# Storing the output of a linear ReLU attention in 2 MB pairs of octets instead of 1 MB octets

## The chip, the cores and the metric

The kernel runs on one NeuronCore of a Trainium2 chip. The metric is the time of the device in microseconds (us). Before the change it is 126.73 us, the median of four executions that lie between 126.46 and 126.92 us. One further execution was taken under the hardware profiler; all the lines of a profile below come from it.

## The reference, cut to what matters

```python
def setup_inputs():
    batch, heads, seq, dim = 8, 12, 512, 64      # Q, K, V: float32, normal random numbers

def reference(Q, K, V):
    Q_feat = np.maximum(0, Q)
    K_feat = np.maximum(0, K)
    KV = np.einsum('bhkd,bhkv->bhdv', K_feat, V)
    K_sum = np.sum(K_feat, axis=2)
    numerator = np.einsum('bhqd,bhdv->bhqv', Q_feat, KV)
    denominator = np.einsum('bhqd,bhd->bhq', Q_feat, K_sum)
    return (numerator / (denominator[:, :, :, None] + 1e-10)).astype(np.float32)
```

There are 96 independent heads. Each has a 64 x 64 matrix KV and a row K_sum, made from its 512 rows of K and V; each of its 512 rows of Q is then multiplied with KV, and divided by its product with K_sum. Three float32 arrays of 12.6 MB are read, one of 12.6 MB is written.

## The kernel before, in words

Heads are taken in *octets*: eight heads at a time, twelve octets (`NO`), numbered `o`. K and V are loaded in half octets of four heads (*groups*, `g` = 2o and 2o + 1). On its 128 partitions an octet of Q has 16 partitions for each head, and each partition holds 32 consecutive rows of 64 numbers, 8 KB in DRAM; a group of K or V has 4 KB on each partition.

**Loads.** All loads but the first two groups are issued by GpSimd (`load_kv`, L92; `load_q`, L98) and change float32 to bfloat16 on the way. They stand in one list at the head of the program, in the order K, V, K, V, Q for each octet (L110 to L113). The pools `qin`, `kin` and `vin` have 7, 12 and 12 buffers. The first two groups come as float32 through the queues of SP and ACT into buffers of the pool of the output (L103 to L107).

**What is done for one octet**, by engine:

- `prep` (L133) and `prep_v` (L141), once for each group: VectorE (DVE) makes the relu of K in two masked copies (`kf`), and V in two masked copies with a column of ones (`vo`); the second copy of V is made by ACT for even groups and by DVE for odd ones.
- `mm_kv` (L148), once for each group: 16 matmuls on TensorE (PE) accumulate KV and K_sum for four heads in the PSUM tile `ps_kv`. `kvs` (L278) does both groups, and then `evac_kv` (L156): ACT copies them into `kvd`, in four instructions. There are two buffers of `kvd`, of an octet each.
- `qt` (L181): PE transposes Q (two sets of eight, `transp`), ACT takes the relu into `qt_sb` (`relu_q`, L174).
- `denom` (L207): 16 small matmuls with the K_sum columns write `ps_den`; DVE masks (`own`, L213), sums (`den`, L218) and takes the reciprocal (`rec`, L222).
- `out_t` (L193): eight matmuls in two halves give the numerator, transposed; ACT copies each half to `ot_sb` (L203).
- `backs` (L272): two times eight float32 transposes on PE (`back`, L225) bring it back to rows, and DVE multiplies each half with the reciprocals out of PSUM into `o_sb` (`norm`, L232). Then `store`.

The PSUM tiles of `out_t` and `back` share one pool of two buffers (`pou`), so a matmul of the one waits until the other's buffer has been read.

**Order.** The schedule is manual: each engine runs its instructions in the order of the program. Iteration `o` of the loop at L286 is: `kvs(o)`, `prep(2o+2)`, the `backs` of octet o - 1, `denom(o)`, `out_t(o)`, `prep(2o+3)`, `qt(o+1)`. From octet 8 on (`SAME`) `kvs(o+1)` is done ahead of `qt(o+1)`, and the `backs` are those of octet o itself. L303 to L328 are the last two octets, whose order is written out by hand; octet 11 is stored in two halves (L244).

**Stores.** All are issued by SP. Ahead of the store of octet `o` < 7, SP issues a transfer of 128 bytes from `k_sb[2(o+5)]` to `scratch` (L242): it waits until that load has landed, and all that SP issues after it waits with it. So the store of octet o goes out when K group 2(o+5) is there. The pool of the output has 7 buffers of 8 KB on each partition.

Of the kernel before, what the change touches and what calls it, by code (L numbers as in the profile page):

```python
# [10 lines left out]
def kernel(  # L11
# [7 lines left out]
    nc = tc.nc  # L19
    B, H, S, D = Q.shape  # L20
# [5 lines left out]

    R = S * 4 // P
# [6 lines left out]
    DELAY = 5  # L34
# [7 lines left out]
    def pool(name, bufs, **kw):  # L42
        return ctx.enter_context(tc.tile_pool(name=name, bufs=bufs, **kw))

    consts = pool("consts", 1)
    qin = pool("qin", 7)
    kin = pool("kin", 12)
    vin = pool("vin", 12)
    kfp = pool("kfp", 4)
    rcp = pool("rcp", 2)  # L50
    outp = pool("outp", DELAY + 2)
# [8 lines left out]

    Qr, Kr, Vr, Or = view(Q, RQ * D), view(K, R * D), view(V, R * D), view(out, RQ * D)

# [13 lines left out]
    kvf = [consts.tile([P, 8 * 2 * D1], bf16, name=f"kvd{i}") for i in range(NK)]  # L76
    kvd = [x.rearrange("p (h d) -> p h d", h=8) for x in kvf]
# [3 lines left out]
    mask_h = consts.tile([P, 8, 2], fp32, name="mask_h")  # L81

    qt_sb = [consts.tile([P, U, P], bf16, name=f"qt{i}") for i in range(NZ)]
    ps_kv = pkv.tile([P, 2, 256], fp32, name="ps_kv")

    ps_den = pde.tile([P, 2, 256], fp32, name="ps_den")
# [15 lines left out]

    for g in range(F32):  # L103
        kv = outp.tile([P, 2, R, D], fp32, name="kv_first", tag="o_sb")
        k_sb[g], v_sb[g] = kv[:, 0], kv[:, 1]
        nc.sync.dma_start(out=k_sb[g].rearrange("p r d -> p (r d)"), in_=Kr[g])
        nc.scalar.dma_start(out=v_sb[g].rearrange("p r d -> p (r d)"), in_=Vr[g])  # L107
# [23 lines left out]
    kf, ot, rec = {}, {}, {}  # L131
# [24 lines left out]
    def evac_kv(o, gs, share=False):  # L156
        for s in range(2):
            for c in range(2):
                copy = nc.vector.tensor_copy if share and c == 1 else nc.scalar.copy
                copy(  # L160
                    kvd[o % NK][64 * c:64 * c + 64, 4 * gs.start + s:4 * gs.stop:2,
                               c * D1:c * D1 + D1].rearrange(
                        "p (g t) d -> p g t d", t=2),
                    ps_kv[64 * s:64 * s + 64, gs, 0:2 * (D + 2)].rearrange(
                        "p g (t d) -> p g t d", t=2)[:, :, :, c:c + D1])
# [8 lines left out]
    def relu_q(o, i, ps, eng=None):  # L174
        to = qt_sb[o % NZ][:, i * (U // 2):(i + 1) * (U // 2)]
        if eng is nc.vector:
            nc.vector.tensor_scalar(to, ps, scalar1=0.0, scalar2=None, op0=Alu.max)
        else:
            nc.scalar.activation(to, ps, Act.Relu)  # L179
# [6 lines left out]
    def idle(n, o):  # L186
        for i in range(n):
            nc.tensor.matmul(ps_den[:, 1], ident, q_sb[o][:, 2 * i:2 * i + 2, :], start=True, stop=True,
                             skip_group_check=True)

    def out_t(o, halves=range(2)):  # L193
        if halves[0] == 0:
            ot[o] = otp.tile([P, U, 8, 16], fp32, name="ot_sb")
        q = qt_sb[o % NZ].rearrange("p u (h c) -> p u h c", h=8)
        for j in halves:
            ps = pou.tile([P, 4, U, 16], fp32, name="ps_ot", tag="ps_out")
            for i in range(4):
                h = 4 * j + i  # L200
                nc.tensor.matmul(ps[:, i], kvd[o % NK][:, h, 1:2 * D + 1], q[:, :, h, :],  # L201
                                 start=True, stop=True, skip_group_check=True)
            nc.scalar.copy(ot[o][:, :, 4 * j:4 * j + 4], ps.rearrange("p h u c -> p u h c"))  # L203
# [3 lines left out]
    def denom(o):  # L207
        ps = ps_den[:, 0].rearrange("p (u h c) -> p u h c", u=U, h=8)
        for u in range(U):
            nc.tensor.matmul(ps[:, u], qt_sb[o % NZ][:, u, :], kvd[o % NK][:, :, 0:2 * D1:2 * D1 - 1],  # L210
                             start=True, stop=True, skip_group_check=True)
        own = rcp.tile([P, U, 8, 2], fp32, name="own")
        nc.vector.scalar_tensor_tensor(  # L213
            own.rearrange("p u h c -> p u (h c)"), ps.rearrange("p u h c -> p u (h c)"), 1e-10,
            mask_h.rearrange("p h c -> p (h c)").unsqueeze(1).to_broadcast([P, U, 16]),
            op0=Alu.add, op1=Alu.mult)
        den = rcp.tile([P, RQ], fp32, name="den")
        nc.vector.tensor_reduce(out=den.rearrange("p (u c) -> p u c", c=2),  # L218
                                in_=own.rearrange("p u h c -> p u c h"), op=Alu.add,
                                axis=mybir.AxisListType.X)  # L220
        rec[o] = rcp.tile([P, RQ], fp32, name="rec")
        nc.vector.reciprocal(rec[o], den)  # L222


    def back(o, j):  # L225
        ps = pou.tile([P, 16, D], fp32, name="ps_bk", tag="ps_out")
        for v in range(8):
            nc.tensor.transpose(ps[:, 2 * v:2 * v + 2].rearrange("p c d -> p (c d)"),  # L228
                                ot[o][:, 8 * j + v].rearrange("p h c -> p (h c)"), ident32)
        return ps  # L230

    def norm(o, j, ps, o_sb):  # L232
        rs = slice(16 * j, 16 * j + 16)
        nc.vector.tensor_tensor(o_sb[:, rs], ps,  # L234
                                rec[o][:, rs].unsqueeze(2).to_broadcast([P, 16, D]), op=Alu.mult)
# [4 lines left out]
    def store(o, o_sb):  # L240
        if o + DELAY < NO:
            nc.sync.dma_start(out=scratch, in_=k_sb[2 * (o + DELAY)][0:1, 0, :])  # L242
        Ov = Or[o].rearrange("p (r d) -> p r d", d=D)
        if o == NO - 1:  # L244
            for j in range(2):
                rs = slice(RQ // 2 * j, RQ // 2 * (j + 1))
                nc.sync.dma_start(out=Ov[:, rs], in_=o_sb[:, rs])
            return
        nc.sync.dma_start(out=Ov, in_=o_sb)

    def out_tile():
        return outp.tile([P, RQ, D], fp32, name="o_sb", tag="o_sb")
# [7 lines left out]
    for c in range(2):  # L260
        nc.vector.tensor_reduce(out=mask_h[:, :, c], in_=ident32.rearrange("p (h b) -> p h b", h=8),
                                op=Alu.add, axis=mybir.AxisListType.X)
# [9 lines left out]
    def backs(o):  # L272
        o_sb = out_tile()
        for j in range(2):
            norm(o, j, back(o, j), o_sb)
        store(o, o_sb)
# [7 lines left out]

    SAME = NO - 4
    for o in range(NO - 2):  # L286
        if 0 < o <= SAME:
            kvs(o)
        prep(2 * o + 2)
        prep_v(2 * o + 2, nc.scalar)  # L290
        if 0 < o <= SAME:
            backs(o - 1)
        denom(o)
        out_t(o)
# [5 lines left out]
        if o >= SAME:  # L300
            backs(o)

    o = NO - 2  # L303
    g = 2 * NO - 2
    prep(g)
    prep_v(g, nc.vector)
    denom(o)
    out_t(o)
# [5 lines left out]
    o_sb = out_tile()  # L314
    norm(o, 0, back(o, 0), o_sb)
    ps = back(o, 1)
# [4 lines left out]
    norm(o, 1, ps, o_sb)  # L321
    store(o, o_sb)
    idle(5, o + 1)
    out_t(o + 1, (0,))
    denom(o + 1)
    out_t(o + 1, (1,))
    idle(6, o + 1)
    backs(o + 1)  # L328
# [28 lines left out]
```

## Time and profile before

| what | value |
|---|---|
| median of four executions | 126.73 us |
| the profiled execution, its own time | 126.71 us |
| its span, first to last instruction | 124.9 us |
| outside the span | 1.8 us |
| busy: PE, DVE, ACT | 86.7, 80.9, 79.4 us |
| matmuls of `mm_kv`, `back`, `qt`, `out_t`, `denom` | 31.6, 23.0, 15.4, 14.9, 7.5 us |
| DVE: `norm`, `kf`, `vo`, `own`, `den`, `rec` | 28.4, 21.2, 17.9, 5.0, 5.0, 4.2 us |
| ACT: `ot_sb`, `qt`, `kvd`, `vo` | 24.1, 22.4, 18.7, 13.8 us |
| read from and written to HBM | 37.75 and 12.58 MB |
| mean granted clock of TensorE | 0.951 |

The busy times of the engines are sums over the span; the row of the DMA in the 40 slices of the profile gives the share of time in which the 16 DMA engines moved something, and the row below it the bytes that they moved, counted as they lie in SBUF. A load is counted with half its DRAM bytes, since it arrives as bfloat16; a store is counted in full.

### The profile page before, as it was taken

The page shows a single profiled execution, that of the slowest core. Times are in us where ns is not written, and L with a number is a line of the kernel's source. Part 1 is how long each engine was busy: PE and PEld are TensorE (multiplying, and loading weights), DVE is VectorE, ACT ScalarE, POOL GpSimd, SP SyncE. Part 2 cuts the span into 40 slices and gives each one's busy share as a digit, 9 for nine tenths or more (in the row PEclk, how much of TensorE's full clock was granted, in tenths as well). Part 3 has the DMA queues.
Part 4 walks back from the last instruction along what each step waited for, and adds up shares of the span by engine and source line. Part 5 has one row for each costly group of instructions (what it writes and reads, how often), then busy time and mean ns, then how long its engine had stood idle before and what let it go on. Part 6 is the DMA issues. An engine that isn't in the chain of part 4 may idle for free.

```text
span 124.9 us, 2656 instructions
## 1 busy us (share of the span) xinstructions
PE 86.7 (69%) x1067; PEld 78.7 (63%) x1067; DVE 80.9 (65%) x176; ACT 79.4 (64%) x114; POOL 31.6 (25%) x62
## 2 busy tenths in 40 slices
PE   0042287998989899894598499398696598697700
PEld 0041285997878788792597399197685497695500
DVE  2247644749797997979248745939729708979430
ACT  0253369979898998988339557779489256637100
POOL 6902424315254331142133124033122000000000
PEclk9999999999999999999869959999999869999996
DMA  2999999999999999999999999999999999999993
GB/s 105 383 307 214 214 207 210 212 210 214 209 211 212 209 216 337 245 216 307 275 212 276 310 212 247 338 212 226 343 228 218 323 256 217 315 422 420 428 412 134
DMA packets 10748, 32.68 MB, mean 262 GB/s; under 512 B 1392, under 2 KB 1392, under 8 KB 9328
## 3 DMA queue, kind: packets, MB, share of 16 engines
q0 software_dynamic: 8064, 17.83, 74.6%
q1 hardware_dynamic: 2384, 13.63, 27.0%
q10 hardware_dynamic: 288, 1.05, 2.1%
q8 instruction: 8, 0.13, 0.4%
q14 instruction: 4, 0.03, 0.1%
HBM read 37.75 MB, written 12.58 MB: 403 GB/s over the span
## 4 chain that ended last, share of the span: by engine, by line
DMA 34%; DVE 30%; PE 24%; ACT 5%; issue 2%; DVEq 1%; SPq 0%; POOLq 0%; ACTq 0%
DMA v_sb<-in_V_dram 14%; DVE o_sb L234 13%; DMA q_sb<-in_Q_dram 13%; PE ps_kv L150 11%; DMA kv_first<-in_K_dram 7%; PE ps_bk L228 7%; DVE kf L136 5%; PE ps_qt L171 4%; DVE vo L138 3%; ACT kvd L160 2%; DVE vo L145 2%; PE ps_ot L201 2%; DVE den L218 2%; ACT qt L179 2%; DVE rec L222 1%
## 5 line engine op out<-in xcount | busy, mean ns | idle before, releaser
L150 PE MATMUL ps_kv<-vo,kf 128*128 128x132 bf16 x384 | 31.6, 248 | 18.0 <-ACT vo L143 8.1
L150 PEld LDWEIGHTS <-kf 128*128 128x128 bf16 x384 | 29.1, 112 | 19.3 <-DVE vo L138 11.1
L234 DVE TENSOR_TENSOR o_sb<-ps_bk,rec 128x1024 f32<-128x1024 f32 x24 | 28.4, 1220 | 17.6 <-PE ps_bk L228 17.6
L160 ACT CAST kvd<-ps_kv 64x260 bf16<-64x260 f32 (+1 forms) x54 | 18.7, 346 | 20.1 <-PE ps_kv L150 17.2
L203 ACT COPY ot_sb<-ps_ot 128x1024 f32<-128x1024 f32 x24 | 24.1, 1013 | 3.1 <-PE ps_ot L201 2.0
L179 ACT ACTIVATE qt<-ps_qt 128x1024 bf16<-128x1024 bf16 x23 | 22.4, 1026 | 5.0 <-PE ps_qt L171 4.9
L228 PE MATMUL ps_bk<-ident,ot_sb 128*128 128x128 f32 x192 | 23.0, 273 | 0.4 <-ACT ot_sb L203 0.4
L136 DVE TENSOR_SCALAR kf<-k_sb,mask 128x1024 bf16<-128x1024 bf16 x44 | 18.3, 458 | 6.4 <-DMA k_sb<-in_K_dram 6.4
L94 POOL DMA_DIRECT2D k_sb<-in_K_dram x22 | 12.3, 560 | 37.8 <-DMA q_sb<-in_Q_dram 20.7
L228 PEld LDWEIGHTS ps_bk<-ident,ot_sb 128*128 128x128 f32 x192 | 20.8, 141 | 0.7 <-ACT ot_sb L203 0.7
L171 PE MATMUL ps_qt<-ident,q_sb 128*128 128x128 bf16 x192 | 15.4, 244 | 5.9 <-DMA q_sb<-in_Q_dram 5.9
L201 PE MATMUL ps_ot<-qt,kvd 128*128 128x256 bf16 x96 | 14.9, 283 | 5.4 <-DVE o_sb L234 4.7
L171 PEld LDWEIGHTS <-q_sb 128*128 128x128 bf16 x192 | 13.7, 111 | 7.2 <-DMA q_sb<-in_Q_dram 6.7
L96 POOL DMA_DIRECT2D v_sb<-in_V_dram x22 | 12.3, 560 | 17.2 <-DMA k_sb<-in_K_dram 9.2
L201 PEld LDWEIGHTS <-kvd 128*128 128x128 bf16 x96 | 9.2, 100 | 8.5 <-issue 6.3
L138 DVE TENSOR_SCALAR vo<-v_sb,mask 128x1024 bf16<-128x1024 bf16 x22 | 10.6, 484 | 1.6 <-DMA v_sb<-in_V_dram 1.6
L143 ACT ACTIVATE vo<-v_sb,mask 128x1024 bf16<-128x1024 bf16 x10 | 11.5, 1153 | 0.2
L210 PEld LDWEIGHTS <-qt 128*128 128x128 bf16 x192 | 6.9, 97 | 3.5 <-ACT qt L179 2.5
L210 PE MATMUL ps_den<-kvd,qt 128*128 128x16 bf16 x192 | 7.5, 180 | 1.7 <-ACT qt L179 1.6
L100 POOL DMA_DIRECT2D q_sb<-in_Q_dram x12 | 6.5, 542 | 8.4 <-DMA v_sb<-in_V_dram 6.1
L213 DVE SCALAR_TENSOR_TENSOR own<-ps_den,mask_h 128x256 f32<-128x256 f32 x12 | 5.0, 418 | 3.3 <-PE ps_den L210 3.3
L136 DVE TENSOR_SCALAR kf<-kv_first,mask 128x1024 bf16<-128x1024 f32 x4 | 2.9, 757 | 5.1 <-DMA kv_first<-in_K_dram 5.1
(24 smaller groups left out, 28.2 us busy)
## 6 DMA issues: line engine op xcount, KB each, us to landing
out_dram<-o_sb SPq DMA_DIRECT2D x11, 1024.0 KB, 9.0
q_sb<-in_Q_dram POOLq DMA_DIRECT2D x12, 512.0 KB, 14.8
k_sb<-in_K_dram POOLq DMA_DIRECT2D x22, 256.0 KB, 14.1
v_sb<-in_V_dram POOLq DMA_DIRECT2D x22, 256.0 KB, 13.2
kv_first<-in_V_dram ACTq DMA_DIRECT2D x2, 512.0 KB, 7.2
kv_first<-in_K_dram SPq DMA_DIRECT2D x2, 512.0 KB, 6.8
out_dram<-o_sb SPq DMA_DIRECT2D x2, 512.0 KB, 4.2
scratch<-k_sb SPq DMA_DIRECT2D x7, 0.1 KB, 4.8
```

The lines of the kernel that those rows point to most:

```text
L94: nc.gpsimd.dma_start(out=k_sb[g].rearrange("p r d -> p (r d)"), in_=Kr[g])
L136: nc.vector.tensor_scalar(kf[g][:, :, s, :], k_sb[g], scalar1=0.0, scalar2=mask[:, 0, s:s + 1], op0=Alu.max, op1=Alu.mult)
L138: nc.vector.tensor_scalar(vo[g % NB][:, :, 0, 2:D + 2], v_sb[g], scalar1=mask[:, 1, 0:1], scalar2=None, op0=Alu.mult)
L150: nc.tensor.matmul(ps_kv[:, g % 2, 0:2 * (D + 2)].rearrange("p (t d) -> p t d", t=2), kf[g][:, r, :, :].rearrange("p s d -> p (s d)"), vo[ ...
L160: copy(kvd[o % NK][64 * c:64 * c + 64, 4 * gs.start + s:4 * gs.stop:2, c * D1:c * D1 + D1].rearrange("p (g t) d -> p g t d", t=2), ps_kv[6 ...
L171: nc.tensor.transpose(ps[:, u, :], q_sb[o][:, i * (U // 2) + u, :], ident)
L179: nc.scalar.activation(to, ps, Act.Relu)
L201: nc.tensor.matmul(ps[:, i], kvd[o % NK][:, h, 1:2 * D + 1], q[:, :, h, :], start=True, stop=True, skip_group_check=True)
L203: nc.scalar.copy(ot[o][:, :, 4 * j:4 * j + 4], ps.rearrange("p h u c -> p u h c"))
L210: nc.tensor.matmul(ps[:, u], qt_sb[o % NZ][:, u, :], kvd[o % NK][:, :, 0:2 * D1:2 * D1 - 1], start=True, stop=True, skip_group_check=True)
L228: nc.tensor.transpose(ps[:, 2 * v:2 * v + 2].rearrange("p c d -> p (c d)"), ot[o][:, 8 * j + v].rearrange("p h c -> p (h c)"), ident32)
L234: nc.vector.tensor_tensor(o_sb[:, rs], ps, rec[o][:, rs].unsqueeze(2).to_broadcast([P, 16, D]), op=Alu.mult)
```

## The change

Octets 0 to 9 are finished and stored as five *pairs* (`a` = o // 2). A pair is 16 heads on 128 partitions: eight partitions for each head and 64 rows, 16 KB in DRAM, on each partition. The last two octets stay as they were.

- **Loads and `kvs`** keep the layout of the octet. `kvd`, `qt_sb` and `ot_sb` become buffers of a pair, two of each. The relu of `relu_q` now reads every second column of its PSUM tile and writes two groups of 64, so that the columns of both octets lie side by side in `qt_sb`, one set for the even and one for the odd partitions of the old layout (`x` = 0, 1).
- **`out_t`** does the same eight matmuls of 256 columns for an octet, but its columns now come in runs of 8 (before: 16).
- **`denom`** is done twice for a pair, for x = 0 and x = 1, each with 16 matmuls of 32 columns (before: one for each octet, 16 matmuls of 16 columns), and `own` has 512 elements on each partition instead of 256. The sum and reciprocal are now `recip`. A second mask for 16 heads is made at the start, and the zeroing of `kvd` covers tiles of twice the size.
- **`backs`** of pair a has four steps (j = 0 to 3), spread over the two octets that follow: 0 and 1 in the iteration of octet 2a + 2, 2 and 3 in that of octet 2a + 3. Both `denom` of a pair are in its second iteration; the first has none.
- **Stores:** five of 2 MB with rows of 16 KB, then octet 10 and the two halves of octet 11 as before. The transfers that gate them wait for K groups 14, 18 and 22 (pairs 0, 1, 2) and V group 23 (pair 3); pair 4 has none.
- **Pools:** `qin`, `kin`, `vin` have 6, 9, 9 buffers, the output 3 of 16 KB on each partition.
- **The tail** (octet 10) begins with steps 0 and 1 of pair 4, then `denom`, `out_t` and `recip` of octet 10, `prep(22)`, steps 2 and 3 of pair 4 and its store.

The diff, cut to its core:

```diff
-    qin = pool("qin", 7)
-    kin = pool("kin", 12)
-    vin = pool("vin", 12)
+    qin = pool("qin", 6)
+    kin = pool("kin", 9)
+    vin = pool("vin", 9)
...
-    outp = pool("outp", DELAY + 2)
+    recp = pool("recp", 2)
+    outp = pool("outp", 3)
...
+    kvf = [consts.tile([P, 16 * 2 * D1], bf16, name=f"kvd{i}") for i in range(NK)]
...
+    mask_h = {n: consts.tile([P, n, 2], fp32, name=f"mask_h{n}") for n in (8, 16)}
...
+    qt_sb = [consts.tile([P, 2 * U, P], bf16, name=f"qt{i}") for i in range(NZ)]
...
     def relu_q(o, i, ps, eng=None):
-        to = qt_sb[o % NZ][:, i * (U // 2):(i + 1) * (U // 2)]
+        us = slice(i * (U // 2), (i + 1) * (U // 2))
+        if paired(o):
+            to = qt_sb[o // 2 % NZ].rearrange("p (x u) f -> p u x f", x=2)[:, us, :, 64 * (o % 2):64 * (o % 2) + 64]
+            ps = ps.rearrange("p u (f x) -> p u x f", x=2)
...
     def out_t(o, halves=range(2)):
...
+            ps = pou.tile([P, 4, 256], fp32, name="ps_ot", tag="ps_out")
+            pv = ps.rearrange("p h (x c) -> p h x c", x=q.shape[1])
...
+                nc.tensor.matmul(pv[:, i], kvd[a % NK][:, h0 + h, 1:2 * D + 1], q[:, :, h, :],
...
+    def denom(o, x, n):
...
         for u in range(U):
+            nc.tensor.matmul(ps[:, u], qt_sb[a % NZ][:, x * U + u, :],
+                             kvd[a % NK][:, h0:h0 + n, 0:2 * D1:2 * D1 - 1],
...
+    def recip(a, x, own):
...
+        nc.vector.reciprocal(rec[a][:, RQ * x:RQ * x + RQ], den)
...
+    def store(a):
+        gate = (k_sb[14], k_sb[18], k_sb[22], v_sb[23], None)[a]
+        if gate is not None:
+            nc.sync.dma_start(out=scratch, in_=gate[0:1, 0, :])
+        nc.sync.dma_start(out=Or2[a], in_=o_sb[a].rearrange("p r d -> p (r d)"))
...
     for o in range(NO - 2):
+        a = o // 2
         if 0 < o <= SAME:
             kvs(o)
         prep(2 * o + 2)
         prep_v(2 * o + 2, nc.scalar)
-        if 0 < o <= SAME:
-            backs(o - 1)
-        denom(o)
-        out_t(o)
+        if o % 2 == 0:
+            if a > 0:
+                backs(a - 1, (0, 1))
+            out_t(o)
+        else:
+            if a > 0:
+                backs(a - 1, (2,))
+            own = denom(o, 0, 16)
+            if a > 0:
+                backs(a - 1, (3,))
+                store(a - 1)
+            recip(a, 0, own)
+            out_t(o, (0,))
+            own = denom(o, 1, 16)
+            out_t(o, (1,))
+            recip(a, 1, own)
         prep(2 * o + 3)
         prep_v(2 * o + 3, nc.vector)
         if o >= SAME:
             kvs(o + 1)
         qt(o + 1)
-        if o >= SAME:
-            backs(o)
 
     o = NO - 2
+    a = o // 2
     g = 2 * NO - 2
+    backs(a - 1, (0, 1))
+    own = denom(o, 0, 8)
+    out_t(o)
+    recip(a, 0, own)
     prep(g)
     prep_v(g, nc.vector)
-    denom(o)
-    out_t(o)
+    backs(a - 1, (2, 3))
+    store(a - 1)
     mm_kv(g)
     evac_kv(o + 1, slice(0, 1))
     prep(g + 1)
     prep_v(g + 1, nc.vector)
```

## The prediction

> **What bounds the kernel now.** I read the page's 40 slices first, then SP's queue, one iteration on DVE and PE in order of time, the clock by stages, and the end.
>
> ```profile
> span 124.9 us, 2656 instructions
> ...
> PE 86.7 (69%) x1067; PEld 78.7 (63%) x1067; DVE 80.9 (65%) x176; ACT 79.4 (64%) x114; POOL 31.6 (25%) x62
> ...
> DMA  2999999999999999999999999999999999999993
> GB/s 105 383 307 214 214 207 210 212 210 214 209 211 212 209 216 337 245 216 307 275 212 276 310 212 247 338 212 226 343 228 218 323 256 217 315 422 420 428 412 134
> ```
>
> The DMA engines are busy from the first slice to the last; each compute engine rests a third of the time. A slice of loads alone shows some 211 GB/s (bytes in SBUF), one of stores alone 412 to 428. An octet of loads is 3 x 0.524 MB in bfloat16, so 7.45 us; a 1 MB store is 2.5 us.
>
> ```profile
> 92.97 0.50 SPq L242 DMA_DIRECT2D scratch<-k_sb  x1
> 93.57 0.53 SPq L249 DMA_DIRECT2D out_dram<-o_sb  x1
> 102.96 0.50 SPq L242 DMA_DIRECT2D scratch<-k_sb  x1
> 103.56 11.28 SPq L249 DMA_DIRECT2D out_dram<-o_sb  x5
> 118.63 1.46 SPq L247 DMA_DIRECT2D out_dram<-o_sb  x2
> ```
>
> SP's gates fall with the landing of K groups 10, 12, ... 22: at 42.76, 52.79, and so on each 10 us (7.45 + 2.5) to 102.96. After that stores drain, and the last half octet, issued at 119.8, lands 4.2 us later. So the end is set by the DMA, with compute close behind: the last two halves are issued while octet 10 is still being stored.
>
> ```profile
> 40.85 2.36 DVE L234 TENSOR_TENSOR o_sb<-ps_bk,rec 128x1024 f32<-128x1024 f32 x2 [0.89 <-PE ps_bk L228]
> 43.12 0.42 DVE L213 SCALAR_TENSOR_TENSOR own<-ps_den,mask_h 128x256 f32<-128x256 f32 x1
> 43.57 0.42 DVE L218 TENSOR_REDUCE den<-own 128x32 f32<-128x256 f32 x1
> 44.03 0.35 DVE L222 RECIPROCAL rec<-den 128x32 f32<-128x32 f32 x1
> 44.30 0.79 DVE L136 TENSOR_SCALAR kf<-k_sb,mask 128x1024 bf16<-128x1024 bf16 x2
> 45.80 0.87 DVE L136 TENSOR_SCALAR kf<-k_sb,mask 128x1024 bf16<-128x1024 bf16 x2
> 47.95 1.22 DVE L234 TENSOR_TENSOR o_sb<-ps_bk,rec 128x1024 f32<-128x1024 f32 x1 [0.88 <-PE ps_bk L228]
> ```
>
> This is an iteration that waits for no load. It lasts 7.1 us, and DVE paces it: two norms of 1.18, own, den, rec 0.45 + 0.46 + 0.27, the prep of the odd group 1.5, that of the even group 1.27, and then 0.9 for `back` on PE. So compute alone does an octet in 7.1 us, less than the loads' 7.45. From 47 on it waits for loads, until about 81.
>
> ```profile
> 97.60:99.10 1.50, 0.00 (x0) 0.97 1.03 340
> 99.10:102.50 3.40, 3.39 (x33) 0.51 1.07 291
> ```
>
> PE alone: busy time, granted clock, DMA share, GB/s. After a PE gap of 1.5 us half the clock is granted; 16 matmuls of L150 take 1.92 us then and 1.11 else, those of `qt` 1.79 and 1.06.
>
> **The change, part by part.**
>
> *Stores.* 10.5 MB now go in rows of 16 KB. A half octet (4 KB rows, 119 to 122 us) moves at 411 GB/s by a share of 0.99, so 415; 8 KB rows (114 to 119) at 426 by 1.01, so 422. Doubling again saves half of that step, 0.8% of 24.9 us: 0.2 us; the whole step, 0.4, is the upper end, and nothing (rows cut up again) the lower. Three gating transfers and five completions less: at most 0.1. If the DMA still sets the end, the time is 126.71 - 0.3 = 126.4; the profiled execution stands 0.02 below the median.
>
> [...]
>
> *Gates and loads.* Until K group 14 no store goes: it lands at 42.76 + 2 x 7.45 = 57.7 (before 62.99), group 18 at 77.6 (15 us of loads, 5 us of a 2 MB store), 20 at 90.0, 22 at 97.5, against 92.97 and 102.96. The loads gain 5.4 us and 2 MB more are left to drain: nothing in total, but the compute tail can start earlier. POOL: K group g needs `prep(g-9)`; 22 needs 13, done by about 67, and is issued some 15 us before landing, so nothing is late. SP: behind the gate on V 23 stand stores of octets not yet finished.
>
> *Compute, odd octets.* `denom` and `recip` of both halves now fall into one iteration. From 256 (418 ns) to 1024 elements (norm, 1220 ns) DVE takes 1.04 ns each, so 512 cost 0.27 more than 256: own 0.72, den 0.73, rec 0.27. Counted from the end of `kvs`: back 0.9, norm 1.18 (to 2.1); `evac_kv` (1.57) and `denom` (0.58) to 2.2; own to 2.95; norm (its `back` stood behind `denom` on PE) to 4.35; den, rec to 5.35; own, den, rec to 7.05; the odd prep 1.5 to 8.55; `mm_kv` 1.1: 9.7 us.
>
> *Compute, even octets.* DVE has only the preps and norms, and PE leads: the second `out_t` half waits for the second norm (3.3), ends 3.9, `qt` 4.9, two `mm_kv` 6.9. A pair takes 16.6 us, before 14.2: 8.3 for an octet, more than the loads' 7.45, less than the 9.95 with stores. DVE's sum in it rises by 1.08 (2 x 1.72 instead of 2 x 1.18). Cover is gone from 35 us on: compute no longer waits for loads.
>
> *Other forms.* A relu reading every second PSUM column, `out_t` in runs of 8, 32 columns in `denom`: elements are the same or few, so I take nothing; no reason allows a gain. Upper ends: a relu at half rate (+0.9 each), 16 small matmuls +0.12. The start: two reductions for the mask (0.48) and a doubled memset (0.50) ahead of the first `evac_kv`, +1.0; with both `denom` in octet 1, `kvs(2)` ends at 34.8 instead of 32.8. `qin`, output and PSUM buffers come free in time: `o_sb` of pair 5 needs the store of pair 2, landed by 109, wanted at 113.
>
> *The end, added up.* `kvs(8)` ends at 34.8 + 3 x 16.6 = 84.6 (before 83.8). Two norms 87.9, prep(19) 89.4; PE: `kvs(9)` 90.7, `qt(9)` 91.75, `back` 92.65. prep(20) waits for K 20 and V 20, to 91.7, under that. ACT: evac and relu to 94.25. Norm 93.85; `denom` 94.65; own 95.4; norm 96.75; den, rec 97.75; own, den, rec 99.45; prep(21) 100.95 (before 99.06). `mm_kv` 102.1, `qt` 103.1, `back` 104.0, two norms 106.4, rec of octet 10 107.6, prep(22) 109.1, **two more norms 111.5**, prep(23) 113.0. These two (2.4 us) are what the tail of before did not have there: octet 8 was finished earlier, in a wait. From prep(23) to the last norm before took 110.1 to 119.75, so it ends at 122.65 and the last half is issued at 122.7. The DMA has then drained nearly all else: stores of pair 3 to 113.7, pair 4 (issued 111.5) to 118.7, octet 10 to 121.2. Its landing takes at least its 1.25 us of data and at most the 4.2 of before, which held 2.9 of backlog; 2.6 lies between and nearer to the unburdened end. 125.3, plus 0.9 to the end of the span, plus 1.8: 128.0.
>
> *The clock.* PE stands idle 2.5 us ahead of `mm_kv(21)`. Three gaps of 1.5 to 2.6 us in the trace (ending at 60.7, 70.9, 99.1) were followed by half clock, one (80.9) not: up to 0.8 + 0.7 more, at least 0.7 if the dip comes a little later. I take it, with 0.8: **128.8**.
>
> [...]
>
> **The rivals.**
>
> *Compute takes the end* (the forecast): 127.3 to 130.
>
> *The DMA keeps it (other side): 126.1 to 126.6.* The place is the last half octet: the drain would reach it at about 122.4, so it decides if the issue comes before some 121.3, 1.4 earlier than I add up, clock dip included 2.2. For it: the slices all at 9, a K 22 that lands 5.4 us sooner, and the idle 4.5 us of DVE ahead of the norms at 103.57, into which work could slip. Against it: DVE runs in order. Whether it is then faster hangs on the 0.2 to 0.4 of the rows. If 16 KB rows are moved as shorter ones, the change does not do what it says and 126.7 remains.
>
> *The strided relu makes ACT the bound: 131.5.* ACT's pair is 2 x 1.57 + 2 x 1.15 + 4 x 1.04 + 4 x 0.98 = 13.5 us; at half rate 17.2, 0.6 over the 16.6, three times, and 0.9 in the tail: 2.7 over the forecast. Against it: L203 takes 1.01 us although it scatters its output.
>
> **How the numbers follow.** Compute at the end 0.62, DMA 0.25, ACT 0.13. A difference under 0.3% (0.4 us) cannot be told from no change. Faster 0.14 and same 0.11 are the DMA's case, split by the row term; slower is the rest. The range goes from the DMA's 126.1 nearly to ACT's case, 131.2; the forecast's own is 127.3 to 130.
>
> **What would show it.** Right: GB/s drops below 400 in the slices before the last, DVE's gap ahead of its norms stays while it has two norms between prep(22) and prep(23), and the last half lands under 3.5 us after its issue. Odd octets of 9.7 and even of 6.9 us between 35 and 80, `own` of 690 ns. Wrong: stores at 420 GB/s to the last slice, the final norm before 121, or relus of ACT far from 1.03 us.

## The result, and the profile after

| | before | after |
|---|---|---|
| median of all executions | 126.76 us (57, 126.39 to 127.24) | 128.07 us (38, 126.43 to 129.40) |
| profiled execution: time, span | 126.71, 124.9 us | 129.40, 127.6 us |

The ratio of the times is 1.0057, with a 95% interval of 1.0041 to 1.0072: slower by 0.7 us. That comparison leaves out executions more than 1.5% above the fastest; here these (128.4 us and more) are not a disturbance from outside but, as will be seen, the kernel's own, and with all of them the medians stand 1.0%, or 1.3 us, apart. The first thing to notice is the spread: the kernel before stays within 0.9 us, the changed one within 3.0.

The page of the changed kernel, in 40 slices of its span:

```profile
span 127.6 us, 2613 instructions
...
PEclk9999999995999999999999999999967779999995
DMA  3999999999999999999999999999999999979644
GB/s 95 361 316 216 214 207 209 214 208 217 204 218 205 210 211 213 212 211 211 303 372 287 215 207 209 259 376 331 209 212 209 216 402 420 447 324 411 280 202 196
...
DVE 36%; PE 27%; ACT 20%; DMA 7%; issue 5%; DVEq 1%; SPq 0%; ACTq 0%
```

Before, the DMA row was 9 to the last slice but one and the stores ran at 412 to 428 GB/s to the end. Now both fall away five slices before the end. The last line is the chain of work that ended last: the DMA has 7% of it, and the three compute engines have 83%. The same line before:

```profile
DMA 34%; DVE 30%; PE 24%; ACT 5%; issue 2%; DVEq 1%; SPq 0%; POOLq 0%; ACTq 0%
```

So the end is no longer set by the DMA but by the compute chain. Where it waits shows in DVE's rows near the end, in order of time:

```profile
100.40 0.48 DVE L151 TENSOR_SCALAR vo<-v_sb,mask 128x1024 bf16<-128x1024 bf16 x1
105.27 2.36 DVE L263 TENSOR_TENSOR o_sb<-ps_bk,rec 128x1024 f32<-128x1024 f32 x2 [4.39 <-PE ps_bk L255]
...
110.20 2.35 DVE L263 TENSOR_TENSOR o_sb<-ps_bk,rec 128x1024 f32<-128x1024 f32 x2
112.47 0.87 DVE L142 TENSOR_SCALAR kf<-k_sb,mask 128x1024 bf16<-128x1024 bf16 x2
...
121.32 2.36 DVE L263 TENSOR_TENSOR o_sb<-ps_bk,rec 128x1024 f32<-128x1024 f32 x2 [1.64 <-PE ps_bk L255]
```

DVE waits 4.39 us after the prep of group 21, because `mm_kv(21)`, `qt` and `back` come only then; the two norms of octet 9's pair stand between the preps of groups 22 and 23, and the last norm ends at 123.68. The stores have nothing to move by then. SP's queue, in order of time:

```profile
97.96 0.51 SPq L276 DMA_DIRECT2D scratch<-k_sb  x1
...
103.69 9.22 SPq L277 DMA_DIRECT2D out_dram<-o_sb  x2
118.45 5.59 SPq L283 DMA_DIRECT2D out_dram<-o_sb  x3
```

Of the page's DMA issues, the row of the last octet's halves (KB each, and us from issue to landing):

```profile
out_dram<-o_sb SPq DMA_DIRECT2D x2, 512.0 KB, 2.7
```

The gate on K group 22 opens at 97.96, against 102.96 before: the loads gained the 5 us that the later stores leave them. The halves of the last octet land 2.7 us after their issue (before 4.2), since no backlog stands ahead of them: from 122 to 124 us the DMA's share is 0.34.

The granted clock of TensorE takes part. In the same trace, four stretches. Each line has the stretch and its length, then the busy time (and the count) of PE, PEld, DVE, ACT and POOL, and at the end the granted clock, the DMA's share and its GB/s:

```profile
90.34:93.75 3.41, 2.07 (x31) 1.70 (x29) 2.50 (x4) 3.36 (x6) 1.05 (x2) 1.00 1.12 213
93.75:97.16 3.41, 3.41 (x32) 3.00 (x30) 2.33 (x3) 1.34 (x2) 0.00 (x0) 0.50 1.08 208
97.16:100.58 3.42, 1.35 (x20) 1.22 (x18) 3.32 (x9) 1.24 (x2) 0.00 (x0) 1.00 1.12 210
100.58:103.99 3.41, 3.06 (x29) 3.06 (x29) 0.30 (x1) 1.08 (x3) 0.00 (x0) 0.50 1.10 323
```

Twice in the tail, for 3.41 us each, half the clock is granted, the second time just under `mm_kv(21)`, `qt` and `back`, for which DVE waits.

### The profile page after: what moved, and what is told of

Read it like the earlier page. It is cut to its first block, busy times and chain, and to the rows that moved or that the text cites. A ratio compares the mean times of both kernels' runs of the same rounds, so it can differ in the third digit from the quotient of the medians.

```text
span 127.6 us, 2613 instructions
## 1 busy us (share of the span) xinstructions
PE 85.5 (67%) x1067; PEld 78.0 (61%) x1067; DVE 87.7 (69%) x178; ACT 78.8 (62%) x114; POOL 32.0 (25%) x62
## 4 chain that ended last, share of the span: by engine, by line
DVE 36%; PE 27%; ACT 20%; DMA 7%; issue 5%; DVEq 1%; SPq 0%; ACTq 0%
DVE o_sb L263 16%; PE ps_kv L156 10%; PE ps_bk L255 8%; ACT qt L191 8%; DMA kv_first<-in_K_dram 7%; ACT kvd L167 7%; DVE kf L142 5%; ACT ot_sb L222 5%; DVE den L244 4%; PE ps_den L232 3%; PE ps_ot L220 3%; DVE own L236 3%; PE ps_qt L178 3%; DVE vo L144 2%; DVE rec L249 2%
## 5 line engine op out<-in xcount | busy, mean ns | idle before, releaser
L156 PE MATMUL ps_kv<-vo,kf 128*128 128x132 bf16 x384 | 28.5, 235 | 22.1 <-ACT vo L149 8.5
L156 PEld LDWEIGHTS <-kf 128*128 128x128 bf16 x384 | 26.2, 104 | 22.9 <-DVE vo L144 10.6
L263 DVE TENSOR_TENSOR o_sb<-ps_bk,rec 128x1024 f32<-128x1024 f32 x24 | 28.7, 1221 | 15.9 <-PE ps_bk L255 15.9
L167 ACT CAST kvd<-ps_kv 64x260 bf16<-64x260 f32 (+1 forms) x54 | 18.7, 345 | 22.1 <-PE ps_kv L156 18.6
L255 PE MATMUL ps_bk<-ident,ot_sb 128*128 128x128 f32 x192 | 25.0, 281 | 0.6 <-ACT ot_sb L222 0.4
L191 ACT ACTIVATE qt<-ps_qt 128x1024 bf16<-128x1024 bf16 x23 | 22.4, 1030 | 0.1
L255 PEld LDWEIGHTS ps_bk<-ident,ot_sb 128*128 128x128 f32 x192 | 21.4, 144 | 1.7 <-ACT ot_sb L222 1.1
L142 DVE TENSOR_SCALAR kf<-k_sb,mask 128x1024 bf16<-128x1024 bf16 x44 | 18.8, 468 | 1.9 <-DMA k_sb<-in_K_dram 1.9
L178 PE MATMUL ps_qt<-ident,q_sb 128*128 128x128 bf16 x192 | 14.7, 237 | 0.0
L232 PE MATMUL ps_den<-kvd,qt 128*128 128x32 bf16 (+1 forms) x192 | 9.3, 199 | 6.3 <-ACT kvd L167 4.5
L232 PEld LDWEIGHTS <-qt 128*128 128x128 bf16 x192 | 8.6, 102 | 7.8 <-issue 5.5
L236 DVE SCALAR_TENSOR_TENSOR own<-ps_den,mask_h 128x512 f32<-128x512 f32 (+1 forms) x12 | 7.4, 620 | 7.7 <-PE ps_den L232 7.7
L244 DVE TENSOR_REDUCE den<-own 128x32 f32<-128x512 f32 (+1 forms) x12 | 7.7, 639 | 0.3
```

The costliest lines, as they stand in the source:

```text
L142: nc.vector.tensor_scalar(kf[g][:, :, s, :], k_sb[g], scalar1=0.0, scalar2=mask[:, 0, s:s + 1], op0=Alu.max, op1=Alu.mult)
L156: nc.tensor.matmul(ps_kv[:, g % 2, 0:2 * (D + 2)].rearrange("p (t d) -> p t d", t=2), kf[g][:, r, :, :].rearrange("p s d -> p (s d)"), vo[ ...
L167: copy(kvd[o // 2 % NK][64 * c:64 * c + 64, h0 + 4 * gs.start + s:h0 + 4 * gs.stop:2, c * D1:c * D1 + D1].rearrange("p (g t) d -> p g t d" ...
L178: nc.tensor.transpose(ps[:, u, :], q_sb[o][:, i * (U // 2) + u, :], ident)
L232: nc.tensor.matmul(ps[:, u], qt_sb[a % NZ][:, x * U + u, :], kvd[a % NK][:, h0:h0 + n, 0:2 * D1:2 * D1 - 1], start=True, stop=True, skip_g ...
L263: nc.vector.tensor_tensor(o_sb[a][:, rs], ps, rec[a][:, rs].unsqueeze(2).to_broadcast([P, 16, D]), op=Alu.mult)
```

## The experiments

Two theories at first. **A**: the compute chain in DVE's order, from the start of the program to the last norm, sets the end; the clock only moves it. **B**: the new form of the stores (2 MB, 16 KB rows, fewer gates) drains worse. All kernels below are edits of the changed kernel; the kernel before ran beside each group of them (126.74, 126.81 and 126.69 us in the three groups).

**1. The changed kernel again.** No edit.

> The changed kernel again, unaltered, for a second look at its profile. Theory A (the chain of compute sets the end, and the half-clock windows of TensorE that fall on it make its time vary): the last half octet is again issued after the DMA engines have run dry, its time spreads over 126.4 to 129.4 us with the place of the half-clock windows, and a faster execution shows the same order of work with a shorter start or tail. Theory B (the DMA sets the end, through rows of 16 KB or the later gates): the DMA engines are busy to the last microsecond and the time is always the same within 0.3 us.

Measured: 127.87 us (ten runs, 126.65 to 128.77), ratio 1.0065 (1.0026 to 1.0104). The profiled execution took 128.17 us, and no half clock falls into its work after 24.8 us. Its DVE rows:

```profile
100.58 0.48 DVE L151 TENSOR_SCALAR vo<-v_sb,mask 128x1024 bf16<-128x1024 bf16 x1
104.03 2.35 DVE L263 TENSOR_TENSOR o_sb<-ps_bk,rec 128x1024 f32<-128x1024 f32 x2 [2.97 <-PE ps_bk L255]
...
120.09 2.36 DVE L263 TENSOR_TENSOR o_sb<-ps_bk,rec 128x1024 f32<-128x1024 f32 x2 [1.65 <-PE ps_bk L255]
```

With the full clock the wait is 2.97 us and not 4.39, and the last norm ends at 122.45. The stores stand still meanwhile, as the same kind of lines shows for this trace:

```profile
118.00:120.00 2.00, 1.55 (x15) 1.25 (x14) 0.41 (x2) 0.90 (x1) 0.00 (x0) 1.00 1.01 422
120.00:122.00 2.00, 0.92 (x9) 0.69 (x7) 1.91 (x2) 0.00 (x0) 0.00 (x0) 1.00 0.29 119
122.00:124.00 2.00, 0.00 (x0) 0.00 (x0) 0.44 (x1) 0.00 (x0) 0.00 (x0) 0.94 0.93 375
```

This is A: the DMA has run dry before the last half octet is ready.

**2. Each 2 MB store as two of 1 MB with 8 KB rows.**

```diff
-        nc.sync.dma_start(out=Or2[a], in_=o_sb[a].rearrange("p r d -> p (r d)"))
+        Ov = Or2[a].rearrange("p (r d) -> p r d", d=D)
+        for x in range(2):
+            rs = slice(RQ * x, RQ * x + RQ)
+            nc.sync.dma_start(out=Ov[:, rs], in_=o_sb[a][:, rs])
```

> Each 2 MB store is issued as two transfers of 1 MB with rows of 8 KB (half of each partition's 16 KB); all compute and the gates stay. Theory A: no change beyond 0.3 us against the changed kernel, since the end waits for compute. Theory B: if rows of 16 KB are what costs, it gets faster by over 0.5 us; if they are worth what the prediction took (0.2 to 0.4 us), it gets slower by that.

Measured: 128.79 us (eight runs, 127.34 to 129.75), ratio 1.0113 (1.0074 to 1.0152). It is no faster, so of B the size and the rows fall; the fewer gates, which this run keeps, are left to run 5. That its median lies 0.9 above run 1 was expected by neither theory. In its profiled execution (128.02 us) the last norm ends at 121.41, but the last half then takes 3.7 us to land: in that trace an instruction fetch of 0.31 us comes at 123.57, in the middle of it, and one of the 16 DMA engines is done at 124.69 where the others are at 123.70 to 123.86; in run 1 the fetch came at 126.70, after the landing. By the granted clock on record for each execution (see "What moves the clock") those of run 2 lie about 1 us above those of the changed kernel with as many stretches of half clock: with one 127.99 and 128.02 (there 126.56 to 127.01), with two 129.75 twice (there 128.41 to 128.87), with none 127.34 to 129.29 (there 126.43 to 128.32). A landing that is late in every execution would do that, but only one trace shows it.

**3. Idle matmuls in the tail.** Six ahead of `denom(9, 0)`, twelve between `mm_kv(20)` and `mm_kv(21)`, so that TensorE isn't idle there.

```diff
+        if o == NO - 2:
+            idle(8, o - 1)
+            idle(4, o - 1)
...
+            if o == NO - 3:
+                idle(6, o)
```

> Eighteen idle matmuls of 256 columns fill two gaps of TensorE in the iteration of octet 9 (6 ahead of the denominators, 12 between the two matmul groups of K and V for octet 10); nothing else is changed and their results are not used. Theory A with the clock: the half-clock windows at about 94 and 101 us vanish, the executions above 128.4 us vanish with them, and the median falls by 0.5 to 1.5 us. Theory A without the clock, or theory B: no change, or slower by what the extra matmuls delay (at most 1 us).

Measured: 128.13 us (four runs, 128.12 to 128.14), ratio 1.0103 (1.0072 to 1.0135). The times above 128.4 are gone, but so are those below 128, and the median did not fall. The profiled execution has the same clock as run 1's, full from 24.6 us on, and the same last norm (ends at 122.41): with no half clock in the tail the idle matmuls neither gain nor cost anything. Four runs so alike settle little about the spread.

**4. Two norms left out**, those of octet 9 between the preps of groups 22 and 23, with zeros from GpSimd in their place.

```diff
+        if a == 4 and j >= 2:
+            nc.gpsimd.memset(o_sb[a][:, rs], 0.0)
+            return
```

> The last two multiplications of pair 4 (1024 elements each, between the preparation of K groups 22 and 23) are left out; GpSimd writes zeros in their place, so the second half of that pair's output is not computed. The transposes ahead of them stay. Theory A: the final multiplications end 2.4 us earlier and the time falls by 1 to 2.4 us, down to the floor of the DMA, 126.1 to 126.5 us, in all executions. Theory B: no change beyond 0.3 us.

Measured: 127.27 us (ten runs, 126.25 to 127.83), ratio 1.0019 (0.9986 to 1.0051): 0.6 less than run 1, where the two norms are 2.36 us of DVE. Its DVE rows, to be held against run 1's (the edit moves lines behind it by three):

```profile
103.56 2.36 DVE L266 TENSOR_TENSOR o_sb<-ps_bk,rec 128x1024 f32<-128x1024 f32 x2 [2.97 <-PE ps_bk L255]
...
111.42 1.23 DVE L266 TENSOR_TENSOR o_sb<-ps_bk,rec 128x1024 f32<-128x1024 f32 x1 [1.25 <-PE ps_bk L255]
...
119.21 2.35 DVE L266 TENSOR_TENSOR o_sb<-ps_bk,rec 128x1024 f32<-128x1024 f32 x2 [1.64 <-PE ps_bk L255]
```

From the norm of 103.56 to the end of the last one it is 18.00 us, in run 1 (104.03 to 122.45) 18.42. So the two norms cost 0.4 us of the chain and not 2.4. A wait of 1.25 us for PE's `back` stands in their place, and more follows: PE and ACT had been nearly as late as DVE.

**5. The odd octets' prep ahead of the reciprocals.** Nothing else: the same stores, gates and instructions.

```diff
+            prep(2 * o + 3)
+            prep_v(2 * o + 3, nc.vector)
             recip(a, 0, own)
...
-        prep(2 * o + 3)
-        prep_v(2 * o + 3, nc.vector)
+        if o % 2 == 0:
+            prep(2 * o + 3)
+            prep_v(2 * o + 3, nc.vector)
```

> In odd octets the preparation of the second K and V group stands ahead of the sums and reciprocals on VectorE instead of behind them; no instruction is added or left out, and the stores and gates are those of the changed kernel. Theory A (the chain of compute, in VectorE's order, sets the end): the second group's matmuls of octet 10 start some 3 us earlier, the wait of VectorE ahead of the multiplications of pair 4 shrinks from 3 to 4.4 us to about 1, an odd octet takes about 8.5 us instead of 9.7, the final multiplication ends at about 120 instead of 122.5, and the time falls to the floor of the DMA, 126.1 to 126.6 us, with a spread of no more than 0.6 us. Theory B (the DMA, through rows or gates): no change against the changed kernel.

Measured: **126.50 us** (twelve runs, 126.20 to 126.68), ratio to the kernel before 0.9976 (0.9966 to 0.9987). An order on one engine takes away more than the change had lost, and most of the spread. In the changed kernel PE waits in each pair for DVE's prep of the odd group. PE's rows in run 1, in order of time:

```profile
47.68 1.11 PE L156 MATMUL ps_kv<-vo,kf 128*128 128x132 bf16 x16
50.48 1.11 PE L156 MATMUL ps_kv<-vo,kf 128*128 128x132 bf16 x16 [1.69 <-DVE vo L151]
```

The same stretch of PE with the early prep, where both groups' matmuls run in one piece:

```profile
45.50 1.06 PE L178 MATMUL ps_qt<-ident,q_sb 128*128 128x128 bf16 x16
46.39 2.06 PE L156 MATMUL ps_kv<-vo,kf 128*128 128x132 bf16 x32
48.29 1.91 PE L255 MATMUL ps_bk<-ident,ot_sb 128*128 128x128 f32 x16
```

A pair takes 15.6 us instead of 16.55 (the first norms of a pair at 34.67, 50.25, 65.82, 81.38), the wait of 2.97 us in the tail is 0.34, and the last norm ends at 117.96. DVE's rows:

```profile
99.10 2.36 DVE L263 TENSOR_TENSOR o_sb<-ps_bk,rec 128x1024 f32<-128x1024 f32 x2 [0.34 <-PE ps_bk L255]
...
108.67 1.23 DVE L263 TENSOR_TENSOR o_sb<-ps_bk,rec 128x1024 f32<-128x1024 f32 x1 [0.71 <-DMA out_dram<-o_sb]
...
115.60 2.36 DVE L263 TENSOR_TENSOR o_sb<-ps_bk,rec 128x1024 f32<-128x1024 f32 x2 [1.65 <-PE ps_bk L255]
```

Now the DMA is the bound again, here in the slices of its page and the landing of its last halves:

```profile
GB/s 103 394 308 211 215 207 209 214 209 216 205 213 210 208 218 207 213 208 208 259 379 337 211 215 207 214 340 371 257 215 206 213 269 419 427 411 427 419 409 120
...
out_dram<-o_sb SPq DMA_DIRECT2D x2, 512.0 KB, 5.3
```

DVE even waits 0.71 us for a store that has to free a buffer. With the very stores and gates of the change the time is 126.5, so neither is what made it slower, and the rest of B falls.

**6. A start with TensorE at work.** 28 idle matmuls of 128 columns between `mm_kv(0)` and `mm_kv(1)`.

```diff
+    for _ in range(28):
+        nc.tensor.matmul(ps_den[:, 256:384], ident, ident, start=True, stop=True, skip_group_check=True)
```

> 28 idle matmuls of 128 columns fill the wait of TensorE at the start (10.4 to 15.7 us), so that its clock is at full when the first transposes and products of Q come; nothing else is changed and their results are not used. If the spread of the changed kernel comes from the clock at its start (kvs of octet 2 ends at 33 to 35 us), the executions at 127.6 to 128.3 us become 126.6 to 127.3, and the median falls by about 1 us; executions with a half-clock window near 100 us stay slower by 0.7 to 1.5. If the start doesn't matter, the distribution stays that of the changed kernel.

Measured: 127.78 us, but the four runs are two pairs: 126.44 and 126.56, 128.99 and 129.23. The profiled one (126.56) has its first pair of norms at 34.38 (run 1: 35.96) and no half clock after 19.4; its last norm ends at 120.85. The start is worth 1.6 us in this trace, and comes out whole at the end. The other two can't be told from it: inconclusive.

**7. An earlier start by order.** `zero_kv(0)` goes ahead of the second group's prep; the masks, the float32 identity and `zero_kv(1)` go behind the preps of octet 0.

```diff
+        if g == 1:
+            zero_kv(0)
...
-    nc.vector.tensor_copy(ident32, ident)
...
-    for k in range(NK):
-        zero_kv(k)
...
+        if o == 0:
+            late_consts()
```

> The zeroing of the first pair's K-V tile stands ahead of the preparation of group 1, in a wait of VectorE, and the masks, the float32 identity and the second tile's zeroing come after the first octet's preparations; all else is the changed kernel's. Theory A: the first copies of K-V to SBUF start at about 10.4 us instead of 14.6, and as compute waits for no load between 30 and 90 us, the whole chain moves ahead by 2 to 3.3 us: the final multiplication ends at 119.5 to 120.5 and the time falls to 126.1 to 126.8 us. Theory B, or if the chain catches up with the loads: no change.

Measured: 126.72 us (ten runs; eight of 126.47 to 126.95, two of 128.3 to 128.4), ratio 1.0008 (0.9982 to 1.0033). The first pair of norms stands at 32.32, 3.6 us before run 1's. By 90.27 the chain has caught up with the loads, and DVE waits for K group 20:

```profile
90.27 0.88 DVE L142 TENSOR_SCALAR kf<-k_sb,mask 128x1024 bf16<-128x1024 bf16 x2 [4.33 <-DMA k_sb<-in_K_dram]
```

The last norm ends at 120.31. So of 3.6 us some 1.15 come through (run 1's 127.87 to 126.72), and that is all that the change had lost.

**8. Four pairs instead of five**, octets 8 to 11 as before.

```diff
-        return o < NO - 2
+        return o < NO - 4
...
+        if not paired(o):
...
+            backs(a, (2 * (o % 2), 2 * (o % 2) + 1))
+            store_octet(o, 1)
```

> Only octets 0 to 7 are stored in pairs of 2 MB; octets 8 to 11 are finished and stored as octets, in the order of the kernel before, with the two last steps of pair 3 ahead of octet 8's. Theory A: the two multiplications that stood between the preparations of groups 22 and 23 are gone from the tail, the final multiplication ends 2.4 us earlier, at 120 to 120.5, and the time is 126.2 to 126.7 us. Theory B: as slow as the changed kernel, less a fifth for one pair fewer.

Measured: 127.66 us (nine runs, 127.35 to 130.26), ratio 1.0069 (1.0040 to 1.0098). The expectation was wrong. Its trace (128.80 us) holds all four norms of the last pair together, ahead of prep(20), although K group 20 is there at about 90 (run 7 has its prep at 90.27); and the wait of 2.97 us for PE occurs twice:

```profile
92.46 4.77 DVE L263 TENSOR_TENSOR o_sb<-ps_bk,rec 128x1024 f32<-128x1024 f32 x4 [2.97 <-PE ps_bk L255]
...
104.05 2.36 DVE L263 TENSOR_TENSOR o_sb<-ps_bk,rec 128x1024 f32<-128x1024 f32 x2 [2.97 <-PE ps_bk L255]
```

The work that stood between the last preps has only moved to the front of the same chain.

**9. Early prep and early start together** (5 and 7).

> The early prep of the odd octets and the early start together. If the DMA is what holds the early prep at 126.5 us (its last norms wait for a store's buffer, its halves land 5.3 us after their issue), the start saves nothing more: 126.2 to 126.7, with the stores at 400 GB/s or more to the last slice. If the compute chain still holds some of it, the 3.6 us that the early start won come through in part: below 126.0.

Measured: **126.17 us** (six runs, 126.06 to 126.49), ratio 0.9964 (0.9951 to 0.9976), the best of all. 3 us of start bring another 0.3 by the medians, 0.15 by the ratios. The slices of its page:

```profile
PEclk9999999999999999999995999999985599999998
DMA  3999999999999999999999999999999999999994
GB/s 100 385 308 216 213 208 208 219 203 216 206 210 214 208 221 202 215 208 212 218 351 405 210 216 204 216 334 378 256 214 208 210 247 427 422 438 427 403 398 161
```

The DMA is busy to the end, as in the kernel before. This execution took 126.09 us although half the clock was granted for 6.8 us in its tail (the 5s at 92.6 to 99.4): its last norm ends at 119.61, early enough that the clock does not show in the time.

**10. The early prep with 8 KB rows** (5 and 2).

> The early prep with each 2 MB store cut into two of 1 MB with rows of 8 KB. Here the DMA sets the end, so the rows' price can be read in the time: packets of 8 KB took 315 to 317 ns and those of 16 KB 620, so 10.5 MB of them on 16 queues, 40 packets of 16 KB each, cost 40 x 12 ns = 0.5 us more as 8 KB rows. The prediction's term was 0.2 (0 to 0.4). So 126.7 to 127.0 if the row length is what the early prep gains on the kernel before; 126.5, unchanged, if it is not.

Measured: 126.78 us (twelve runs, 126.57 to 127.29), ratio 1.0012 (0.9996 to 1.0028), against 0.9976 for the 16 KB rows. The difference of the ratios is 0.36%, or 0.45 us; that of the medians 0.28, from two groups of runs. But the rows are not all that differs between the two traces. Stretches of half clock at 53.1, 70.2 and 87.2 bring run 10's last norm to 120.36 (117.96 in run 5), and an instruction fetch of 0.31 us comes at 122.5, while its stores still drain (in run 5 after them, at 124.8). The four executions with as low a granted clock (0.93) lie at 126.98 to 127.29, the other eight have a median of 126.72. So the row length is worth at most 0.2 to 0.45 us where the DMA sets the end, and without it nothing is left of the gain over the kernel before.

**11. The changed kernel a third time**, for another trace.

> The changed kernel once more, for the trace of another execution. If the start's half clock is what differs between its executions, an execution of 126.4 to 127.0 us has its first pair of norms at 34.5 or earlier and its last norm ending before 121.3; one of 128 us or more has the first pair at 35.0 or later. If something at the end makes the difference, the first pair stands at 35.0 to 36.0 in either.

Measured: 129.07 us in the profiled execution, 128.64 in the other. The trace shows the first pair at 35.00 and the half clock at 94.30 and 101.13, as in the first profile of the change. So "35.0 or later" held, but an execution below 127 us was not caught, and the start alone is not what differs: run 1's start was *later* (35.96) and its time shorter.

**12. Idle matmuls in both places** (3 and 6).

> The changed kernel with idle matmuls in both places: 28 of 128 columns ahead of the second K and V group's matmuls, and 6 and 12 ahead of denom(9,0) and of mm_kv(21). If TensorE's half clock at the start and in the tail is what spreads the changed kernel's times from 126.4 to 129.4 us, both gone leave 126.3 to 127.0 in nearly every run. If the spread has another cause, or the idle matmuls only shift the dips, times of 127.5 and more stay.

Measured: 127.06 us (twelve runs, 126.65 to 128.44), ratio 1.0054 (1.0023 to 1.0084). Seven lie at 126.65 to 127.08, but 127.39, 127.79 and three of 128.3 to 128.4 stay: 1.0 us less than the change in the median, and the spread is narrower but not gone. In its trace the half clock has only moved: it comes at 16.4 for 6.8 us, behind the idle matmuls of the start, and the tail has none. "Nearly every run" was wrong.

**What moves the clock.** The record of the granted clock begins with the first full clock; before it matmuls are slow (in run 1, 16 of L156 take 1.92 us at 15.7 and 1.11 at 31.6). In the 14 traces the changes between full and half clock lie whole multiples of 3.413 us apart (the last section has the figures), and at other times of the program in each execution. Eight of them:

| trace | full clock from | half clock for 3.41 us at | first norms of a pair | last norm ends | time |
|---|---|---|---|---|---|
| change, first profile | 18.7 | 28.9, 93.8, 100.6 | 35.01 | 123.68 | 129.40 |
| change again (11) | 19.2 | 29.5, 94.3, 101.1 | 35.00 | 123.37 | 129.07 |
| change again (1) | 24.8 | none | 35.96 | 122.45 | 128.17 |
| change, 8 KB rows (2) | 20.0 | 26.8 | 34.92 | 121.41 | 128.02 |
| warm start (6) | 12.6 | 16.0 | 34.38 | 120.85 | 126.56 |
| early start (7) | 16.2 | 26.4 | 32.32 | 120.31 | 126.74 |
| early prep (5) | 18.4 | 28.7 | 34.67 | 117.96 | 126.24 |
| both (9) | 20.9 | 65.3, 92.6, 96.0 | 31.66 | 119.61 | 126.09 |

Time less the end of the last norm is 5.70 to 5.72 us in the traces of 129.40, 129.07, 128.17 and 126.56: there compute sets the end. With the last norm at 120.31 and before it is 6.4 to 8.3: there the DMA does. (The 6.6 of the 8 KB rows are the late landing told above.) So the time hangs on two things: whether the start and the tail have the full clock in that execution, and whether the last norm comes before some 120.5 us.

Executions without a trace bear this out in part, since the mean granted clock of each is on record (the time before the first full clock counts as full in it). In the traces each stretch of 3.41 us takes some 0.014 off it: 0.990 with none (run 1), 0.971 to 0.974 with one (runs 2, 5, 6 and 7), 0.968 and 0.961 with two (runs 8 and 12), 0.951 and 0.948 with three (run 11 and the first profile). Sorted by it, the 50 executions of the changed kernel fall into four groups; the number of stretches is an estimate from these means:

| mean granted clock | stretches of half clock | executions | time |
|---|---|---|---|
| 0.947 to 0.951 | three | 8 | 128.77 to 129.40 |
| 0.963 to 0.965 | two | 10 | 128.41 to 128.87 |
| 0.974 to 0.976 | one | 7 | 126.56 to 127.01 |
| 0.987 to 0.990 | none | 25 | 126.43 to 128.32 |

Every time above 128.4 has two or three stretches by this estimate. The seven with one agree with the trace of the 8 KB rows, which has one, at the start; its last norm ends at 121.41 and would give 127.1 without the late landing. Where in an execution a stretch fell, the mean does not tell. The 1.9 us between executions with none come from elsewhere; that they come from the moment at which the full clock begins (run 1, at 24.8, is near their upper end) is argued, not shown, as no trace of a short one was caught.

## Why the prediction was right or wrong

The sign, the mechanism and the range held: slower, by compute at the end, and 128.07 lies in 126.1 to 131.2. The size was too large: 128.8 where the median is 128.07 and the ratio means 127.5. **The step that failed is the clock: "I take it, with 0.8: 128.8".**

- **The clock, +0.8.** It was one number added to a chain whose start came from one trace, that of the kernel before, with the first full clock at 23.9 us. Measured, it is of both signs. At the start it is 0 to -1.0 us (first norms at 35.96 in run 1, 35.00 in run 11, 34.92 in run 2). In the tail, from the first norms of pair 3 to the end of the last norm, it is 0 or about +2: 36.84 us in run 1 (85.61 to 122.45), 38.74 in run 11 (84.63 to 123.37), 39.04 in the first profile (84.64 to 123.68). Together -1.0 to +1.2 from one execution to another, against a term of 0.7 to 1.5, always added. The profiled execution of 129.40 lies above the forecast and the median below it, so neither the sign nor the size of that term could stand for all executions. In the granted clock of the 50 executions only 18 have the two or three stretches that go with 128.4 us and more.
- **The sum without the clock, 128.0, held.** Run 1, with the full clock throughout its tail, took 128.17; its last norm ends at 122.45 (worked out: 122.65).
- **Gates, loads.** 57.7, 77.6 and 97.5 were worked out for K groups 14, 18 and 22; measured 58.05, 77.87 and 97.96. The last half was to land after 2.6 us: 2.7.
- **Odd and even octets.** 16.6 for a pair, 16.55 measured (norms at 35.01, 51.55, 68.10 and 84.64). `own` of 512 elements: 660 ns in the mean (the first of a pair 690, the second 630), forecast 690 from the slope between two shapes.
- **"Two more norms", 2.4 us.** Their place was right, their price was not: run 4 gives 0.4 us. The sum came out since PE and ACT, which it took to be covered there, were as late; removing DVE's work leaves PE's `back` as the next wait. This is a wrong reason behind a right sum, and it didn't show until work was taken out.
- **Row length, 0.2 (0 to 0.4).** At most 0.2 to 0.45 by run 10, its upper half. The DMA's case ends at 126.2 to 126.5 (runs 5 and 9), where 126.1 to 126.6 was given to it as a rival.
- **The rival "the DMA keeps it".** True of runs 5 and 9 to the tenth, once the chain was made shorter. Its threshold was given as an issue before 121.3; measured, the last norm ends at 120.31 in run 7, where the DMA has the end, and at 120.85 in run 6, where compute has it, so the change lies at some 120.5.
- **The rival of a slow relu** falls: the strided relu on ACT takes 1030 ns a piece, the row it was costed by. Of the other forms taken at nothing, the 16 matmuls of `denom` take 0.77 us instead of 0.58, 0.19 more where 0.12 was the upper end.
- **What would show it.** The slices below 400, DVE's gap ahead of its norms, the landing below 3.5 us and the octets of 9.7 and 6.9 all appear (9.8 and 6.7 from the ends of `kvs` at 40.8, 50.6 and 57.3). None of the three signs against it did in the first profile.

So where did the expected gain of the longer rows and the gates go? It is there, 0.2 to 0.45 us of rows at the DMA at most and 5 us at the last gate, but the loads that came earlier met a compute chain that needs 16.55 us for each pair (against 14.2) and has no wait for loads left to hide it.

## What to carry to other kernels

A change that joins iterations to make a transfer larger lengthens the stretch of each engine's order between a load and the work that frees the next one: add up the pair as one iteration in that order, and look first for independent work standing behind a long chain of small steps; here 1.6 us of prep moved ahead of 2.6 us of masks, sums and reciprocals was worth more than the row length. Once compute took the end from the DMA here, TensorE's clock and the program's start, hidden until then, came into the time, so a range and not one number belongs to them. A price for work that is late on one engine holds only if the next engine is not as late; the run that leaves it out tells.

## What the runs showed of the hardware that was not expected

- **Changes of the clock at multiples of 3.413 us.** From 23.90 us on, TensorE's granted clock before the change is full and half in turn for 37.55, 3.41, 6.83, 3.41, 23.90, 3.41 and 20.48 us; in the first profile of the change, from 18.66 us on, for 10.24, 3.41, 61.44, 3.41, 3.42, 3.41 and 20.48 us. These are 11, 1, 2, 1, 7, 1 and 6, and 3, 1, 18, 1, 1, 1 and 6 times 3.413 us. Up to 118 us all 14 traces can be divided into stretches of 3.413 us in each of which the clock is 1.00 or 0.50 throughout; the first of them begins from 0.01 to 3.40 us after the start of the span, at another time in each execution. The same kernel has no half clock in its work after 25 us in run 1 and three stretches in the first profile (128.17 and 129.40 us).
- **Half clock after a stretch with PE partly busy.** Of these stretches with full clock, between 20 and 117 us in the 14 traces, ahead of the end of the work, all nine in which PE was busy for less than 1.5 of the 3.41 us were followed by half clock (0.81 to 1.46 us busy); of the 67 with 1.51 to 2.21 us, 11 were (the line of 90.34 above: 2.07 us busy, then 0.50); of the 289 with more, none.
- **Rows.** In the means of the traces, store packets of 16 KB took 620 ns (run 1) and those of 8 KB 315 to 317 (runs 2 and 10, the kernel before), so two of 8 KB took some 12 ns more than one of 16 KB. Over the 10.5 MB (40 packets of 16 KB on each of 16 engines) that is 0.5 us, a little above the 0.2 to 0.45 us of run 10.
- **An instruction fetch in the drain.** In run 2's trace a fetch of 0.31 us on one DMA engine went with that engine ending its last store 0.83 us after the other fifteen (124.69 against 123.86 at the latest).
